# Chunk states of a scan layer from three products of rounded parts, with GpSimd's work for a chunk reordered

## The chip, the cores and the metric

The kernel runs on one core of a Trainium2 chip. The metric is device time in microseconds (us) of one execution of the whole program; lower is better. The engines of the core are called as the profile calls them: PE (TensorE, matrix products), PEld (its weight loads), DVE (VectorE), ACT (ScalarE), POOL (GpSimd) and SP (SyncE, which issues most DMAs). Each engine works through its own queue of instructions in order and waits for others by semaphores.

## The reference

A decoder trunk of two layers on 1040 tokens (16 meta tokens and 1024 inputs) of width 1024. The first layer is a Mamba-2 scan mixer and a gated FFN, the second an attention and a gated FFN. The change lies in the scan mixer. With chunks of the sequence, per group g of 8 heads (4 groups, 32 heads of 64 columns, a state of 128):

```python
xdt = x_c * dt_c[..., None]
y_diag = einsum('bgcls,bgecls,bcsgep->bclgep', cb, decay_in, xdt)
decay_to_end = exp(a_cs[..., -1:] - a_cs)
chunk_states = einsum('bclgn,bgecl,bclgep->cbgepn', b_c, decay_to_end, xdt)
def step(state, inp):
    s_new, d = inp
    return state * d[..., None, None] + s_new, state
y_off = einsum('bclgn,cbgepn,bgecl->bclgep', c_c, prev_states, exp(a_cs))
y = y_diag + y_off
```

In words: within a chunk every token takes up the earlier ones through a decay (`y_diag`); each chunk leaves a state, the product of `b_c` with its inputs times `dt` times the decay to the end of the chunk (`chunk_states`); the state that came into a chunk is read by the queries `c_c` times a decay (`y_off`).

## The kernel before

Everything is float32. Large products are made of three products of rounded parts: a value is split into a high part of type float32r and a low part (the value less its high part), and `mm3` adds high x high, high x low and low x high in one PSUM bank. In the trace these are lines 209, 210 and 211. A product of two float32 tiles that is given to PE directly shows as two records of one instruction.

The sequence is cut into 9 chunks of 116 tokens (the last of 112), and for the projections into 3 token tiles of 348, 348 and 344. The scan runs group by group (0 to 3), and in a group chunk by chunk, in `mixer`. Between the two halves of a chunk's work stand **units** of the input projections: one unit is one block of 128 output columns for one token tile, 24 products on PE. `next(work)` issues a unit. How many units go to a chunk is in `SHARES`: two in groups 0 and 3 (with exceptions at the first and last chunk), four, three and three in turn in groups 1 and 2. A block has three units; ahead of its first unit the next block's weights are split, by a copy on ACT (L196) and four subtractions on POOL (`wl`, L102). A unit of the convolved columns is evicted by ACT (L336) and then by three taps on DVE (L339), and a unit later by a Silu on ACT (L616). A unit of the gate columns is evicted by a Silu on ACT (L648), multiplied in on DVE (L655), and squared a unit later (ACT L660, DVE L664 or L666). Units write in turn to two banks `mm` and one bank `ex`.

For PE, DVE, ACT and POOL the order of all this is the order in which the Python code issues it (`manual_schedule`). Per chunk it is:

- `ssd_decays` (L735), a generator in three steps for the *next* chunk: the DMAs of its decays `D` and `E` by SP; then eight subtractions on DVE (L754) and an Exp on ACT (L755); then, but for chunk 0, `E` times the queries on POOL in four pieces (`E`, L102). Each `next(work)` but the first of a chunk takes one more step, so that with two units the DMAs and the Exp are issued among the units, and with three units the POOL step as well. What is left is taken when the next chunk begins.
- `ssd_front` (L761): on PE a transpose and a product into `cb` (L771, L772) and four transposes into `px` (L775); on ACT the copy `bk` (L780); on DVE `cbm` (L782), `xdt` (L784) and `D*cbm` (L785); on POOL the decayed inputs `xde` in two pieces (L102).
- the units.
- `ssd_back` (L791): on PE the chunk states `S` from `bk` and `xde` (L801), then for each head the products with `D` (L812) and with `E` and the incoming state (L814); on DVE the addition to the state (L807) and the skip connection (L816); on POOL the state times the next chunk's decay (`state`, L102).

The ninth chunk has no `S`, `bk` and `xde`: 32 chunks have them.

Of the kernel before, what the change touches and what calls it, by code (L numbers as in the profile page):

```python
# [8 lines left out]
F32 = mybir.dt.float32  # L9
F32R = mybir.dt.float32r  # L10
AF = mybir.ActivationFunctionType
ALU = mybir.AluOpType

P = 128
# [7 lines left out]
CH = [(c * CB, min(CB, L - c * CB)) for c in range(9)]  # L22
# [32 lines left out]
GH = 8  # L55
# [36 lines left out]
def pieces(eng, out, x, y, op):  # L92

    n = out.shape[1]
    size = 1
    for d in out.shape[2:]:
        size *= d
    step = max(1, PIECE // size)
    done = []
    for a in range(0, n, step):  # L100
        c = slice(a, min(a + step, n))
        done.append(eng.tensor_tensor(out[:, c], x[:, c], y[:, c], op=op))  # L102
    return done


class Trunk:
# [628 lines left out]
    def ssd_decays(self, g, ct, c, pool):  # L735

        nc = self.nc
        h0 = GH * g
        t0, n = CH[c]
        cc = 3 * (c % 3) + c // 3  # L740
        dk = pool.tile([P, 1024], F32, tag="D", name=self.nm("D"))
        dk = dk[:n, : GH * CB].rearrange("p (h l) -> p h l", h=GH)
        nc.sync.dma_start(dk, self.acs_d[c, h0 : h0 + GH].unsqueeze(0).to_broadcast([n, GH, CB]))
        dk = dk[:, :, :n]
        ce = None
        if c:
            ce = pool.tile([P, GH * CB], F32, tag="E", name=self.nm("E"), bufs=2)
            ce = ce.rearrange("p (h l) -> p h l", h=GH)
            nc.sync.dma_start(ce, self.ea_d[c, h0 : h0 + GH].unsqueeze(0).to_broadcast([P, GH, CB]))
            ce = ce[:, :, :n]  # L750
        yield dk, ce

        for i in range(GH):
            nc.vector.tensor_scalar(dk[:, i], dk[:, i], self.cols[:n, 1, cc, h0 + i : h0 + i + 1], 0.0, op0=ALU.subtract, op1=ALU.min)  # L754
        nc.scalar.activation(dk, dk, AF.Exp)  # L755
        yield
        if c:
            pieces(nc.gpsimd, ce, ce, ct[:, t0 : t0 + n].unsqueeze(1).to_broadcast([P, GH, n]), ALU.mult)
        yield

    def ssd_front(self, g, x, bt, ct, c, dk, pool):  # L761

        nc = self.nc
        h0 = GH * g
        tt = nc.vector.tensor_tensor
        t0, n = CH[c]
        cc = 3 * (c % 3) + c // 3
        e = t0 + n
        pcb = self.sm("cb")
        if c < 8:  # L770
            nc.tensor.transpose(pcb[:n, P : 2 * P], bt[:, t0:e], self.ident)  # L771
        nc.tensor.matmul(pcb[:n, :n], bt[:, t0:e], ct[:, t0:e], start=True, stop=True)  # L772
        px = self.lg("px")
        for q in range(4):
            nc.tensor.transpose(px[:n, q * P : q * P + P], x[q][:, t0:e], self.ident)  # L775
        px = px[:n].rearrange("p (h d) -> p h d", h=GH)
        bk = xde = None
        if c < 8:
            bk = pool.tile([P, P], F32, tag="bk", name=self.nm("bk"), bufs=2)
            nc.scalar.activation(bk[:n], pcb[:n, P : 2 * P], AF.Copy)  # L780
        cbm = pool.tile([P, CB], F32, tag="cbm", name=self.nm("cbm"), bufs=2)
        tt(cbm[:n, :n], pcb[:n, :n], self.past[:n, :n], op=ALU.mult)  # L782
        xdt = pool.tile([P, GH, 64], F32, tag="xdt", name=self.nm("xdt"), bufs=2)
        tt(xdt[:n], px, self.cols[:n, 0, cc, h0 : h0 + GH].unsqueeze(2).to_broadcast([n, GH, 64]), op=ALU.mult)  # L784
        tt(dk, dk, cbm[:n, :n].unsqueeze(1).to_broadcast([n, GH, n]), op=ALU.mult)  # L785
        if c < 8:
            xde = pool.tile([P, GH, 64], F32, tag="xde", name=self.nm("xde"), bufs=2)
            pieces(nc.gpsimd, xde[:n], xdt[:n], self.cols[:n, 2, cc, h0 : h0 + GH].unsqueeze(2).to_broadcast([n, GH, 64]), ALU.mult)
        return xdt, xde, bk

    def ssd_back(self, g, x, c, dk, ce, xdt, xde, bk, states, pool):  # L791

        nc = self.nc
        h0 = GH * g
        t0, n = CH[c]
        cc = 3 * (c % 3) + c // 3
        e = t0 + n
        state, new = states
        if c < 8:
            ps = self.lg("S")  # L800
            nc.tensor.matmul(ps, bk[:n], xde[:n].rearrange("p h d -> p (h d)"), start=True, stop=True)  # L801
            psv = ps.rearrange("p (h d) -> p h d", h=GH)
            if c == 0:
                new = pool.tile([P, GH, 64], F32, tag="state", name=self.nm("state"), bufs=2)
                nc.scalar.activation(new, psv, AF.Copy)
            else:
                nc.vector.tensor_tensor(new, new, psv, op=ALU.add)  # L807
        py = self.sm("y")
        for i in range(GH):
            q, r = i // 2, 64 * (i % 2)  # L810
            y = py[r : r + 64, q * CB : q * CB + n]
            nc.tensor.matmul(y, xdt[:n, i, :], dk[:, i, :], start=True, stop=c == 0)  # L812
            if c:
                nc.tensor.matmul(y, state[:, i, :], ce[:, i, :], start=False, stop=True)  # L814
        for q in range(4):
            nc.vector.scalar_tensor_tensor(x[q][:, t0:e], x[q][:, t0:e], self.par("d_skip", 4 * g + q),  # L816
                                           py[:, q * CB : q * CB + n], op0=ALU.mult, op1=ALU.add)
        scaled = None
        if c < 7:
            scaled = pool.tile([P, GH, 64], F32, tag="state", name=self.nm("state"), bufs=2)  # L820
            cn = 3 * ((c + 1) % 3) + (c + 1) // 3
            pieces(nc.gpsimd, scaled, new, self.cd[:, cn, h0 : h0 + GH].unsqueeze(2).to_broadcast([P, GH, 64]), ALU.mult)
        return new, scaled

    def mixer(self, mx):


        with self.tc.tile_pool(name="start", bufs=3) as pool:
            u, dt, heads, w0, front = self.load_x(pool, mx, self.a["w_in"][DI // P])
# [8 lines left out]
        with self.tc.tile_pool(name="ssd", bufs=3) as pool:  # L838
# [27 lines left out]
            with self.tc.manual_schedule(engines={E.PE, E.DVE, E.Activation, E.Pool}):  # L866
                ahead = self.ssd_decays(0, rows[0][5], 0, pool)
                dk, ce = next(ahead)
                for g in range(GROUPS):
                    *x, bt, ct = rows[g]  # L870
                    share, given = SHARES[g], 0
                    state = None, None
                    for c in range(9):
                        if g == c == 0:
                            next(work)
                            given = 1
                        for _ in ahead:
                            pass
                        begun = False
                        ops = self.ssd_front(g, x, bt, ct, c, dk, pool)  # L880
                        now = dk, ce
                        for _ in range(sum(share[: c + 1]) - given):
                            next(work)
                            if not begun:
                                begun = True
                                nxt = (g, ct, c + 1) if c < 8 else (g + 1, rows[g + 1][5], 0) if g < 3 else None
                                ahead = self.ssd_decays(*nxt, pool) if nxt else iter([(None, None)])
                                dk, ce = next(ahead)
                            else:
                                next(ahead, None)  # L890
                            given += 1
                        state = self.ssd_back(g, x, c, *now, *ops, state, pool)
                        if g == 3:
                            done.append(c)
                            todo, waiting[:] = waiting[:], []
                            for w in todo:
                                later(*w)
                            if c == 7:
                                self.gate_factors()
                                y0 = self.fetch_y(yd[0])  # L900
                next(work)
                r = [self.tmp("r0") for _ in TT]
                for t, (s0, n) in zip(r, TT):
                    self.nc.sync.dma_start(t[:, :n], self.gr_d[0:1, s0 : s0 + n].to_broadcast([P, n]))
                y0 = y0, [self.Q("yh", F32R) for _ in y0]
                for j in range(3):
                    self.split_y(0, *y0, j, r[j])
                    next(work, None)
                for _ in work:
                    pass  # L910
# [1156 lines left out]
```

## Time and profile before

| | |
|---|---|
| median of 3 runs | 2845.09 us (2844.49 to 2850.29) |
| the profiled execution's own time | 2848.77 us |
| its span, from first to last instruction | 2847.0 us |
| mean granted clock of PE | 0.997 |
| PE busy | 2806.7 us |
| DVE, ACT, POOL busy | 2071.6, 1582.8, 1572.9 us |
| `S` (L801), records and mean of one | 64, 598 ns |
| the scan's groups, from first to last `S` | 122.57 to 596.41 us |

How to read its lines. In a timeline a line has the start in us from the span's start, the time in us, the engine, the line of code and the operation, the tile that is written and those that are read (`S<-xde,bk`), the shapes, and a count when several like it are taken together; in square brackets stands how long the engine had been idle before it, and what ended that. Line 102 is the helper that cuts POOL's work into pieces, lines 209 to 211 are `mm3`: there the tile's name says which work it is. The type that is printed for products of rounded parts is f32 too. `ACT_TABLE_LOAD` loads the table of the function that the line names. In a view by stretches the columns are the stretch, its length, the busy us (and instructions) of PE, PEld, DVE, ACT and POOL, the granted clock, the share of the DMA engines and GB/s. In a view of waits a line has the engine and what it was about to do, what it waited for, the sum in us, how often, and the longest.

### The profile page before, as it was taken

The numbers are of one execution on the slowest core, as the hardware profiler recorded it, in microseconds if no ns is written. First come the engines' busy times: TensorE is split into PE (matmuls) and PEld (weight loads), VectorE is DVE, ScalarE is ACT, GpSimd is POOL, SyncE is SP. The second block draws the span as 40 slices with busy tenths as digits, with TensorE's granted clock in tenths as the row PEclk, the third lists the DMA queues.
The fourth block names the chain that finished last, engine by engine and source line by source line (L and its number), as shares of the span: only waits on it lengthen the run. The fifth ranks groups of instructions, "written<-read, shape, count | busy, mean of one in ns | idle before, by whom it ended". The sixth has DMA issues, their size and how long they took to land. (4 is left out here: it accounts for less than half of the span.)

```text
span 2847.0 us, 56457 instructions
## 1 busy us (share of the span) xinstructions
PE 2806.7 (99%) x21251; PEld 2690.8 (95%) x21251; DVE 2071.6 (73%) x3936; ACT 1582.8 (56%) x3077; POOL 1572.9 (55%) x2144
## 2 busy tenths in 40 slices
PE   8999999999999999999999999999999999999998
PEld 7989999999999999999999999999898999999888
DVE  5676666668487676767886888888759676667786
ACT  5555554543256565655335777777646555555433
POOL 2366455553519888867763111112354888886881
PEclk9999999999999999999999999999999999999999
DMA  4333333343412222235142222322532222225331
GB/s 119 88 112 97 116 84 124 117 137 101 116 68 95 78 79 79 78 129 181 44 153 75 77 67 71 85 70 55 186 132 82 83 75 82 75 83 185 111 104 67
DMA packets 141740, 281.78 MB, mean 99 GB/s; under 512 B 16307, under 2 KB 71740, under 8 KB 141468
## 3 DMA queue, kind: packets, MB, share of 16 engines
q1 hardware_dynamic: 135844, 267.01, 29.6%
q0 software_dynamic: 2048, 6.49, 0.6%
q10 hardware_dynamic: 3576, 4.67, 0.5%
q8 instruction: 168, 2.75, 0.4%
q14 instruction: 104, 0.85, 0.1%
HBM read 207.79 MB, written 55.42 MB: 92 GB/s over the span
## 5 line engine op out<-in xcount | busy, mean ns | idle before, releaser
L102 POOL TENSOR_TENSOR wl<-w,wh 128x256 fp32r<-128x256 f32 x760 | 676.3, 921 | 345.4 <-ACT wh L196 225.8
L209 PE MATMUL pj<-uh,wh 128*128 128x348 f32 (+2 forms) x1536 | 501.1, 327 | 3.4 <-DVE xbc L339 1.4
L210 PE MATMUL pj<-ul,wh 128*128 128x348 f32 (+2 forms) x1536 | 494.8, 322 | 0.8 <-DVE ul L320 0.8
L211 PE MATMUL pj<-uh,wl 128*128 128x348 f32 (+2 forms) x1536 | 491.9, 320 | 0.0
L209 PE MATMUL p<-bh,fh 128*128 128x262 f32 (+1 forms) x1408 | 401.6, 285 | 7.1 <-DVE p L1239 3.7
L211 PE MATMUL p<-bh,fl 128*128 128x262 f32 (+1 forms) x1408 | 401.4, 285 | 0.9 <-POOL fl L102 0.9
L210 PE MATMUL p<-bl,fh 128*128 128x262 f32 (+1 forms) x1408 | 399.6, 284 | 0.1
L102 POOL TENSOR_TENSOR fl<-x,fh 128x256 fp32r<-128x256 f32 x352 | 263.6, 783 | 192.9 <-ACT fh L1176 167.0
L210 PE MATMUL p<-bl,wh 128*128 128x262 f32 (+1 forms) x1040 | 295.6, 284 | 1.1 <-DVE bl L1100 1.1
L209 PEld LDWEIGHTS pj<-uh,wh 128*128 128x128 f32 x1536 | 288.7, 188 | 7.5 <-DVE qs L1607 3.1
L209 PE MATMUL p<-bh,wh 128*128 128x262 f32 (+1 forms) x1040 | 295.4, 284 | 0.4 <-ACT ft L1236 0.4
L211 PE MATMUL p<-bh,wl 128*128 128x262 f32 (+1 forms) x1040 | 294.3, 283 | 0.0
L210 PEld LDWEIGHTS pj<-ul,wh 128*128 128x128 f32 x1536 | 289.2, 188 | 2.4 <-DVE ul L320 1.4
L339 DVE SCALAR_TENSOR_TENSOR c<-p,params,c 128x260 f32<-128x260 f32 (+1 forms) x528 | 248.4, 480 | 57.4 <-ACT c L336 50.9
L211 PEld LDWEIGHTS pj<-uh,wl 128*128 128x128 f32 x1536 | 288.7, 188 | 0.1
L209 PEld LDWEIGHTS p<-bh,fh 128*128 128x128 f32 x1408 | 268.5, 191 | 8.1 <-DVE p L1239 4.1
L211 PEld LDWEIGHTS p<-bh,fl 128*128 128x128 f32 x1408 | 267.6, 190 | 1.7 <-POOL fl L102 1.3
L210 PEld LDWEIGHTS p<-bl,fh 128*128 128x128 f32 x1408 | 268.4, 191 | 0.5 <-DVE bl L1100 0.3
L1236 ACT ACTIVATE ft<-p 128x262 f32<-128x262 f32 (+1 forms) x352 | 133.6, 382 | 180.9 <-DVE p L1239 110.9
L210 PE MATMUL acc<-gl,wh 128*128 128x260 f32 (+1 forms) x672 | 214.2, 320 | 0.0
L211 PE MATMUL acc<-gh,wl 128*128 128x260 f32 (+1 forms) x672 | 213.2, 319 | 0.0
L209 PE MATMUL acc<-gh,wh 128*128 128x260 f32 (+1 forms) x672 | 210.8, 320 | 0.1
(337 smaller groups left out, 7689.2 us busy)
## 6 DMA issues: line engine op xcount, KB each, us to landing
w<-in_w_up SPq DMA_DIRECT2D x88, 512.0 KB
w<-in_w_down SPq DMA_DIRECT2D x44, 512.0 KB
w<-in_w_in SPq DMA_DIRECT2D x40, 512.0 KB
E<-ea_d SPq DMA_DIRECT2D x32, 464.0 KB
D<-acs_d SPq DMA_DIRECT2D x32, 420.5 KB
g<-c SPq DMA_DIRECT2D x88, 130.0 KB
g<-c SPq DMA_DIRECT2D x88, 128.0 KB
b<-g SPq DMA_DIRECT2D x16, 520.0 KB
```

The costliest lines, as they stand in the source:

```text
L102: done.append(eng.tensor_tensor(out[:, c], x[:, c], y[:, c], op=op))
L209: self.behind(mm(out, wh, uh, start=first, stop=False, skip_group_check=joins), tie, "behind the sums of squares")
L210: mm(out, wh, ul, start=False, stop=False, skip_group_check=joins)
L211: self.last_mm = mm(out, wl, uh, start=False, stop=last, skip_group_check=joins)
L339: ins = nc.vector.scalar_tensor_tensor(out, ps[:, o + i : o + i + n], wcol(i), out, op0=ALU.mult, op1=ALU.add)
L1236: nc.scalar.activation(s[:, :N], ps[:, :N], AF.Copy)
```

## The change

The chunk states' product of two float32 tiles becomes three products of rounded parts. `bk` becomes two tiles side by side, a high part from ACT and a low part from DVE; `xde` is split after POOL has made it, by a copy on ACT and a subtraction on DVE (`split_xde`). The buffers of `bk` and `xde` go from two to one each, with one for each part. Besides, `ssd_decays` now tells when its Exp has been issued; what is left of it when a chunk begins, POOL's `E`, is issued after `ssd_front`, so after `xde`, and not before. If the Exp is still outstanding then, that step is taken first.

```diff
@@ ssd_decays
         nc.scalar.activation(dk, dk, AF.Exp)
-        yield
+        yield "decays"
         if c:
             pieces(nc.gpsimd, ce, ce, ct[:, t0 : t0 + n].unsqueeze(1).to_broadcast([P, GH, n]), ALU.mult)
         yield
@@ ssd_front
         if c < 8:
-            bk = pool.tile([P, P], F32, tag="bk", name=self.nm("bk"), bufs=2)
-            nc.scalar.activation(bk[:n], pcb[:n, P : 2 * P], AF.Copy)
+            bk = pool.tile([P, 2, P], F32R, tag="bk", name=self.nm("bk"), bufs=1)
+            nc.scalar.activation(bk[:n, 0], pcb[:n, P : 2 * P], AF.Copy)
+            tt(bk[:n, 1], pcb[:n, P : 2 * P], bk[:n, 0].bitcast(F32), op=ALU.subtract)
...
         if c < 8:
-            xde = pool.tile([P, GH, 64], F32, tag="xde", name=self.nm("xde"), bufs=2)
-            pieces(nc.gpsimd, xde[:n], xdt[:n], self.cols[:n, 2, cc, h0 : h0 + GH].unsqueeze(2).to_broadcast([n, GH, 64]), ALU.mult)
+            xde = [pool.tile([P, GH, 64], dt, tag=t, name=self.nm(t), bufs=1) for t, dt in (("xdh", F32R), ("xdl", F32R), ("xde", F32))]
+            pieces(nc.gpsimd, xde[2][:n], xdt[:n], self.cols[:n, 2, cc, h0 : h0 + GH].unsqueeze(2).to_broadcast([n, GH, 64]), ALU.mult)
+            self.split_xde(xde, c)
         return xdt, xde, bk
+
+    def split_xde(self, xde, c):
+
+        hi, lo, t = (t[: CH[c][1]] for t in xde)
+        self.nc.scalar.activation(hi, t, AF.Copy)
+        self.nc.vector.tensor_tensor(lo, t, hi.bitcast(F32), op=ALU.subtract)
@@ ssd_back
             ps = self.lg("S")
-            nc.tensor.matmul(ps, bk[:n], xde[:n].rearrange("p h d -> p (h d)"), start=True, stop=True)
+            hi, lo = (t[:n].rearrange("p h d -> p (h d)") for t in xde[:2])
+            self.mm3(ps, bk[:n, 0], bk[:n, 1], hi, lo, True, True)
@@ mixer
                 dk, ce = next(ahead)
+                decayed = False
...
-                        for _ in ahead:
-                            pass
-                        begun = False
-                        ops = self.ssd_front(g, x, bt, ct, c, dk, pool)
+                        if not decayed:
+                            next(ahead)
+                        begun = False
+                        ops = self.ssd_front(g, x, bt, ct, c, dk, pool)
+                        for _ in ahead:
+                            pass
...
                                 dk, ce = next(ahead)
+                                decayed = nxt is None
                             else:
-                                next(ahead, None)
+                                decayed |= next(ahead, None) == "decays"
```

## Prediction

> **What bounds the kernel now.** I read the head of the page first, then the busy time by stretches, then the waits of PE, and last the timelines of single chunks.
>
> ```profile
> span 2847.0 us, 56457 instructions
> PE 2806.7 (99%) x21251; PEld 2690.8 (95%) x21251; DVE 2071.6 (73%) x3936; ACT 1582.8 (56%) x3077; POOL 1572.9 (55%) x2144
> ```
> ```profile
> 119.00:220.00 101.00, 98.50 (x775) 90.20 (x774) 77.84 (x197) 60.45 (x81) 61.85 (x85) 1.00 0.36 104
> 510.00:612.00 102.00, 101.57 (x787) 93.03 (x787) 64.33 (x158) 54.67 (x83) 71.99 (x96) 1.00 0.39 121
> ```
> ```profile
> PE y L812 <- DVE D L785: 1.5, 1, 1.5
> PE S L801 <- POOL xde L102: 1.5, 3, 0.6
> ```
>
> PE is busy for 99% of the span, at a granted clock of 1.00, so time saved on PE is time saved, and time that PE waits is time lost. The second view gives, for two stretches, length and then PE, PEld, DVE, ACT and POOL; 119 to 220 us is the scan's group 0, 510 to 612 is group 3. No other engine is near full there: DVE is at 77% and 63%, ACT at 60% and 54%. But the third view (PE alone, 115 to 612 us) says that PE does wait a little on the chain which this change lengthens: three times for the decayed inputs `xde`. So the question is not how busy ACT, DVE and POOL are, but how long the chain through them is against what PE does meanwhile.
>
> **The product itself.** One chunk in group 0, and a product of rounded parts with the same 512 columns elsewhere:
>
> ```profile
> 178.95 1.02 PE L801 MATMUL S<-xde,bk 116*128 116x512 f32 x2
> 179.90 0.43 PE L812 MATMUL y<-D,xdt 116*64 116x116 f32 x4
> ...
> 190.22 1.02 PE L801 MATMUL S<-xde,bk 116*128 116x512 f32 x2
> ```
> ```profile
> 2604.50 0.40 PE L209 MATMUL acc<-gh,wh 128*128 128x512 f32 x1
> 2604.73 0.40 PE L210 MATMUL acc<-gl,wh 128*128 128x512 f32 x1
> ```
>
> The f32 product of chunk states holds PE for 179.90 - 178.95 = 0.95 us. Products of rounded parts follow each other at 2604.73 - 2604.50 = 0.23 us, so three hold it for about 0.70. That is 0.25 us less per chunk, for 4 groups of 8 chunks 32 x 0.25 = 8.0 us: the whole possible gain. (If the change-over to the products behind costs the three the same 0.05 us as the old pair, it is 0.20 a chunk, 6.4 in all.) A chunk of group 0 now takes PE 190.22 - 178.95 = 11.27 us; after the change its own work is 11.02.
>
> **What is added, and where it stands.** Per chunk ACT gets one copy of 512 columns (the high part), queued right behind `bk`; DVE gets a subtraction from PSUM of 128 columns (the low part of `bk`), ahead of `cbm`, and one of 512 columns behind `D*cbm`. ACT's copy waits for GpSimd's `xde`, and behind it on ACT stand the next unit's evictions, Silu's table load and Silu itself: these are the ones that a late `xde` now holds up. DVE's 512 columns wait for ACT's copy, and behind them stand the next unit's taps (L339) or gate products (L655). PE's second product waits for them. (A unit is one weight block times one token tile, 24 matmuls.) The rows for the walk, group 0 first:
>
> ```profile
> 183.89 1.19 POOL L102 TENSOR_TENSOR state<-state,cd 128x256 f32<-128x256 f32 x2 [2.30 <-DVE state L807]
> 185.04 3.51 POOL L102 TENSOR_TENSOR E<-E,xbc 128x232 f32<-128x232 f32 x4
> 188.49 1.20 POOL L102 TENSOR_TENSOR xde<-xdt,cols 116x256 f32<-116x256 f32 x2
> ...
> 299.73 2.00 POOL L102 TENSOR_TENSOR xde<-xdt,cols 116x256 f32<-116x256 f32 x2 [0.52 <-DVE xdt L784]
> ```
> ```profile
> 175.31 0.64 ACT L336 ACTIVATE xbc<-pj,params 128x344 f32<-128x344 f32 x1 [2.22 <-PE pj L211]
> 175.97 1.28 ACT L616 ACT_TABLE_LOAD   x1
> ...
> 177.67 1.04 ACT L196 ACTIVATE wh<-w 128x1024 fp32r<-128x1024 f32 x1
> 179.15 0.64 ACT L336 ACTIVATE xbc<-pj,params 128x348 f32<-128x348 f32 x1 [0.44 <-PE pj L211]
> ```
> ```profile
> 179.82 1.81 DVE L339 SCALAR_TENSOR_TENSOR xbc<-pj,params,xbc 128x348 f32<-128x348 f32 x3 [2.04 <-ACT xbc L336]
> 181.55 1.60 DVE L754 TENSOR_SCALAR D<-D,cols 116x116 f32<-116x116 f32 x8
> 183.06 0.68 DVE L807 TENSOR_TENSOR state<-state,S 128x512 f32<-128x512 f32 x1
> 183.66 1.07 DVE L816 SCALAR_TENSOR_TENSOR xbc<-xbc,params,y 128x116 f32<-128x116 f32 x4
> 184.65 0.28 DVE L782 TENSOR_TENSOR cbm<-cb,past 116x116 f32<-116x116 f32 x1
> 184.83 0.69 DVE L784 TENSOR_TENSOR xdt<-px,cols 116x512 f32<-116x512 f32 x1
> ```
>
> Now `xde` runs behind the four `E` pieces and is done at 188.49 + 1.20 = 189.69, half a microsecond ahead of the product at 190.22. With the new order (it takes effect only in groups 0 and 3, two units a chunk; with three units `E` is already made before) `xde` starts when `xdt` ends, 185.5. There it runs beside DVE's `D*cbm`: the row at 299.73 is that case, 2.00 us instead of 1.20. So 187.5 instead of 189.7: 2.2 us earlier, and the two new steps come behind it. `E` follows, 3.5 us, and its last piece is wanted only by the last of the products with the queries.
>
> Unknown prices: the 512-column copy lies between this view's L648 for 348 columns, 0.46, and L196 for 1024, 1.04; by slope 0.60, and I take 0.63 with its start. The 512-column subtraction lies between L655's 0.51 and 1.00 (rows below, 348 columns, POOL idle and POOL busy) and their stretch to 512 columns, 0.75 to 1.4; since `E` runs beside it I take 0.9. The 128-column one is like `cbm`: 184.83 - 184.65 = 0.18. Below nothing none can go, each being an added instruction.
>
> On an unlagged chunk these steps fit: 187.5 + 0.6 + 0.9 = 189.0, product possible at 190.0. But ACT's queue has become part of a **ring** that leads from one `xdt` to the next, and the ring can be longer than PE's 11.02. Step by step: `xdt` 0.74 with its hand-over; `xde` 2.00; copy 0.68; ACT's L336, table load and Silu, 177.67 - 175.31 = 2.36; the second unit's L336 up to DVE's start, 179.82 - 179.15 = 0.67; three taps 181.55 - 179.82 = 1.73; L754 183.06 - 181.55 = 1.51; L807 0.60; L816 0.99; low `bk` 0.18; `cbm` 0.18. Sum 11.64. Besides, the weight split's copy L196 (1.04) stands in two chunks of three: 12.34. Today the ring is open, because ACT waits for PE (2.22 us in the row at 175.31) and its table load hides in that time; the copy waiting ahead of it takes this cover away, so that the 1.28 us come behind `xde`.
>
> Group 0 then goes at 12.34 instead of 11.27: 7 gaps between its 8 products x 1.07 = 7.5 us, less about 0.5 for idle time at the start: **+7**.
>
> Group 3, gates instead of taps:
>
> ```profile
> 522.90 1.94 POOL L102 TENSOR_TENSOR xde<-xdt,cols 116x256 f32<-116x256 f32 x2 [0.33 <-DVE xdt L784]
> 527.37 1.02 PE L801 MATMUL S<-xde,bk 116*128 116x512 f32 x2
> ...
> 561.28 1.02 PE L801 MATMUL S<-xde,bk 116*128 116x512 f32 x2
> 572.36 1.12 PE L801 MATMUL S<-xde,bk 116*128 116x512 f32 x2
> ```
> ```profile
> 561.84 0.48 ACT L660 ACTIVATE z<-xbc 128x348 f32<-128x348 f32 x1
> ...
> 566.42 1.28 ACT L648 ACT_TABLE_LOAD   x1
> 568.77 0.46 ACT L648 ACTIVATE z<-pj 128x344 f32<-128x344 f32 x1 [1.07 <-PE pj L211]
> ```
> ```profile
> 563.20 0.51 DVE L655 TENSOR_TENSOR xbc<-xbc,z 128x348 f32<-128x348 f32 x1
> 563.62 1.60 DVE L754 TENSOR_SCALAR D<-D,cols 116x116 f32<-116x116 f32 x8
> ...
> 570.27 1.00 DVE L655 TENSOR_TENSOR xbc<-xbc,z 128x344 f32<-128x344 f32 x1
> ```
>
> Ring: 0.74 + 2.00 + 0.68; table load 1.30; first unit's L648 to the end of its L655, 571.27 - 568.77 = 2.50; second unit's L660 to L754, 563.62 - 561.84 = 1.78; then 1.51 + 0.60 + 0.99 + 0.36. Sum 12.46, with a third of L196 12.8; with L655 at 0.51, 12.0 to 12.3. I take 12.4, against 572.36 - 561.28 = 11.08 today. This group starts with room: `xde` was done 527.37 - 524.84 = 2.53 ahead of its product, and ACT has a wait for PE in it. I let the first three gaps go free and four pay 1.3: **+5**.
>
> Groups 1 and 2 have three or four units a chunk:
>
> ```profile
> 249.59 0.46 ACT L648 ACTIVATE z<-pj 128x348 f32<-128x348 f32 x1 [3.48 <-PE pj L211]
> ```
> ```profile
> 251.80 1.74 POOL L102 TENSOR_TENSOR xde<-xdt,cols 116x256 f32<-116x256 f32 x2
> ```
> ```profile
> 256.88 1.02 PE L801 MATMUL S<-xde,bk 116*128 116x512 f32 x2
> ```
>
> Here the room between `xde` and product is 256.88 - 253.54 = 3.34 us, in one of the tightest chunks, and copy and subtraction take 0.6 + 0.9. The cost that is hidden here is on ACT: L648 at 249.59 would have to wait for the copy, until about 254.2, 4.6 us. PE does not feel that: a unit writes one of three banks in turn (two of `mm`, one of `ex`), so the bank is wanted again only two units (2 x 3.8 us) and a chunk's own products later. Were this cover gone, each such chunk would lose those us. So these 16 chunks gain: 16 x 0.25 = **-4**.
>
> **Sum:** +7 + 5 - 4 = +8 us. The profiled execution took 2848.77 us, 1.8 us above its span and 3.7 above the median of the runs (2845.09). From the median: 2845 + 8 = **2853 us**. Own range of this case: a copy of 0.5 to 1.0 and L655's two prices move each ring by some 0.4 us, over 11 gaps 4.4; the rings closing a chunk earlier or later is 1.3 each; the dearer subtraction (1.4) adds a little above: 2848 to 2862.
>
> [...] The table load is the largest cover that goes. In the row at 175.97 it takes 1.28 us, and L336, load and Silu together are over 2.36 us after they began, so that nothing stands behind the load. [...]
>
> **Rivals.**
> - *The ring does not close.* If `xde` beside `D*cbm` takes 1.20 instead of 2.00 (as at 188.49) and the table load still hides (Silu's load ahead of the waiting copy), the ring of group 0 is 12.34 - 0.80 - 1.28 = 10.3, under 11.02, that of group 3 likewise, and all 32 chunks gain: 2845 - 7.5 = 2837.5. For it: DVE and ACT are idle a quarter of the time or more. Against it: the rows of `xde` that begin as `xdt` ends, 2.00 at 299.73 and 1.94 at 522.90, and loads that stand directly ahead of the function that needs them.
> - *Break-even.* `xde` alone at 1.20, or L196 hidden beside DVE's work: rings of 11.5 and 11.6, +2 in each group, -4: 2845. For it: L196 in group 3 can lie beside L666 and L655.
> - *The products with the queries wait for the whole of `E`.* After the change `E` ends 3.5 us after `xde`; products with the state begin at 0.6 + 0.9 + 0.47 + 0.25 = 2.2 us after it. By pieces they never wait; if all four are waited for, 1.3 us more in each of 14 chunks: +18, about 2870. It decides as soon as one wait covers all pieces. Against: the pieces are separate instructions on separate heads.
> - *The order does not change:* `xde` stays behind `E`. The ring grows by 3.5 - 0.8 = 2.7 us in 14 chunks: +38, about 2890.
> [...]
>
> **How the numbers follow.** 0.2% (5.7 us) is about what a measurement of this kernel can tell from no change: bounds 2839.4 and 2850.8. Chances: forecast 0.50, not closed 0.22, break-even 0.18, whole `E` 0.06, order 0.02, second wait 0.02. Of the forecast's 0.50, 0.10 lies under 2850.8. So slower 0.40 + 0.10 = 0.50, same 0.18 + 0.10 = 0.28, faster 0.22. The range goes from the not-closed case's 2837 to 2864, which takes in the forecast's own range and leaves out the last three rivals and a little below.
>
> **What would show it.** Right: products S as three of L209 to L211, 0.70 us from first to next; gaps of S in group 0 of 11.7 to 12.4 us, in the later chunks of group 3 of 12 to 13; PE waiting there for ACT's high and DVE's low part, 12 to 20 us in total; `xde` at 2.00 directly behind `xdt`, `E` behind it; ACT's table load directly behind the copy; in groups 1 and 2 no wait of PE and 0.25 us less a chunk. Wrong: gaps of 11.0 in group 0, then the ring has a member that runs beside another; waits of PE in groups 1 and 2, then the banks are no cover; or waits of the state products for `E`.

## The result and the profile after

The changed kernel takes **2871.11 us** (median of 5 runs, 2869.72 to 2873.35), the kernel before beside it 2844.49 (2844.31 to 2850.29): ratio 1.0091, 95% interval 1.0080 to 1.0103. It is slower, as forecast, but by 26.6 us, where +8 was forecast, and above the range's upper end of 2864.

The head of the page after, and PE's waits in the scan (110 to 640 us):

```profile
span 2869.2 us, 56648 instructions
PE 2814.6 (98%) x21283; PEld 2703.3 (94%) x21283; DVE 2109.0 (74%) x4000; ACT 1595.9 (56%) x3109; POOL 1575.2 (55%) x2144
```
```profile
PE S L210 <- DVE xdl L797: 5.5, 11, 0.7
PE pj L209 <- DVE xbc L339: 5.1, 2, 2.5
PE S L209 <- ACT xdh L796: 4.6, 7, 1.3
PE y L821 <- DVE D L786: 3.4, 1, 3.4
PE ms L676 <- DVE z L666: 1.5, 2, 1.0
PE ms L676 <- DVE xbc L825: 0.6, 1, 0.6
```

PE now waits 20.7 us where it waited 3.0: for the two parts of `xde` (10.1), but also at three kinds of place of which the prediction had nothing: twice for DVE's taps ahead of a unit (`pj`), once for `D*cbm` (`y`), and three times, once each in groups 1 to 3, for the sums of squares `ms`.

The starts of `S` in the timelines show where. One row per stretch, us, for both kernels and for the experiments below (e7, which adds waits to the kernel before, is read by itself):

| stretch | before | after | e1 | e2 | e3 | e4 | e5 | e6 | e8 | e9 | e10 |
|---|---|---|---|---|---|---|---|---|---|---|---|
| group 0, first to last S | 78.92 | 86.07 | 76.91 | 78.62 | 85.98 | 78.07 | 99.52 | 82.12 | 78.91 | 84.17 | 89.82 |
| on to group 1's first | 26.59 | 31.41 | 27.26 | 29.11 | 31.18 | 28.65 | 29.92 | 30.03 | 26.60 | 31.72 | 27.07 |
| groups 1 and 2 | 260.02 | 268.41 | 257.53 | 257.53 | 268.59 | 260.03 | 269.44 | 267.45 | 257.55 | 267.83 | 273.49 |
| on to group 3's first | 29.00 | 28.82 | 28.83 | 28.83 | 28.99 | 29.00 | 28.83 | 28.79 | 28.85 | 28.83 | 32.67 |
| group 3, first to last S | 79.31 | 85.45 | 78.46 | 81.69 | 85.35 | 78.45 | 94.47 | 85.95 | 79.30 | 85.31 | 92.16 |

Before to after: +7.2, +4.8, +8.4, -0.2, +6.1, together +26.3. Groups 0 and 3 lose what was forecast (+7 and +5). The other 13 us stand in groups 1 and 2 and at the change from group 0 to group 1.

A chunk of group 0 after the change, by engine (POOL, ACT, DVE):

```profile
195.35 1.94 POOL L102 TENSOR_TENSOR xde<-xdt,cols 116x256 f32<-116x256 f32 x2 [0.76 <-DVE xdt L785]
197.25 3.04 POOL L102 TENSOR_TENSOR E<-E,xbc 128x232 f32<-128x232 f32 x4
```
```profile
197.32 0.63 ACT L796 ACTIVATE xdh<-xde 116x512 fp32r<-116x512 f32 x1 [3.50 <-POOL xde L102]
197.86 0.62 ACT L336 ACTIVATE xbc<-pj,params 128x348 f32<-128x348 f32 x1
198.50 1.28 ACT L616 ACT_TABLE_LOAD   x1
```
```profile
197.98 1.12 DVE L797 TENSOR_TENSOR xdl<-xde,xdh 116x512 fp32r<-116x512 f32 x1 [1.74 <-ACT xdh L796]
199.03 3.62 DVE L339 SCALAR_TENSOR_TENSOR xbc<-pj,params,xbc 128x348 f32<-128x348 f32 x6
202.56 1.60 DVE L754 TENSOR_SCALAR D<-D,cols 116x116 f32<-116x116 f32 x8
```

As forecast, `xde` starts as `xdt` ends and takes 1.94, ACT stands 3.50 us idle at the copy, and L336 and the table load come behind it. The other queue was named in the prediction, but not added up: DVE stands 1.74 us idle at its own new step, and when that is done, the taps of *two* units (`x6`) follow without a gap and lead straight to L754. Both queues are held, not ACT's alone.

PE at such a place, the high part's wait and the low part's:

```profile
198.00 0.50 PE L209 MATMUL S<-xdh,bk 116*128 116x512 f32 x1 [0.58 <-ACT xdh L796]
199.16 0.50 PE L210 MATMUL S<-xdl,bk 116*128 116x512 f32 x1 [0.66 <-DVE xdl L797]
```

And the unforeseen place in group 1, a chunk of four units of convolved columns:

```profile
336.09 0.63 ACT L796 ACTIVATE xdh<-xde 116x512 fp32r<-116x512 f32 x1 [4.54 <-POOL xde L102]
336.63 0.62 ACT L336 ACTIVATE xbc<-pj,params 128x344 f32<-128x344 f32 x1
```
```profile
336.76 0.69 DVE L797 TENSOR_TENSOR xdl<-xde,xdh 116x512 fp32r<-116x512 f32 x1 [1.74 <-ACT xdh L796]
337.37 3.59 DVE L339 SCALAR_TENSOR_TENSOR xbc<-pj,params,xbc 128x344 f32<-128x344 f32 x6
```
```profile
339.30 0.40 PE L209 MATMUL pj<-uh,wh 128*128 128x348 f32 x1 [2.54 <-DVE xbc L339]
```

The first unit's bank is read by ACT's L336 and then by three taps on DVE, and only the last of them sets it free; they end near 339.2, and the fourth unit, which takes the same bank, has been waiting for 2.54 us. Before, the first unit's taps of this chunk stood here:

```profile
315.94 1.80 DVE L339 SCALAR_TENSOR_TENSOR xbc<-pj,params,xbc 128x344 f32<-128x344 f32 x3 [0.35 <-ACT xbc L336]
```

They began 8.3 us behind the last `S` ahead of them (307.66); after the change it is 15.7 us (337.37, `S` at 321.67). Group 2 has the same place at 489.56. These two chunks take 4.1 us more each (23.07 and 23.06 between their starts of `S`, where it was 18.94), and two others 1.0 and 0.6 more, where PE waits for `ms`; the other gaps are a little shorter.

Last, the granted clock. Stretches of after, columns as before, the clock third from the end:

```profile
135.80:149.50 13.70, 13.03 (x90) 12.07 (x91) 10.94 (x26) 8.42 (x12) 10.10 (x14) 0.88 0.40 103
149.50:161.10 11.60, 11.27 (x92) 10.42 (x90) 8.78 (x23) 5.97 (x10) 7.66 (x12) 1.00 0.53 125
...
321.70:344.70 23.00, 20.46 (x139) 19.64 (x139) 19.32 (x40) 10.80 (x17) 13.83 (x20) 0.93 0.27 85
...
573.50:587.00 13.50, 12.83 (x90) 11.84 (x91) 9.29 (x23) 7.99 (x11) 8.08 (x11) 0.87 0.32 84
```
```profile
215.00:230.00 15.00, 11.56 (x81) 10.99 (x80) 11.97 (x36) 5.68 (x7) 2.36 (x5) 0.77 0.59 133
```

Before, the clock was 1.00 all through the scan. Now five stretches lie below, each behind a wait of PE, or behind two waits close together (0.70 and 0.67 us up to 136.95, 1.03 and 0.66 up to 574.67); the fifth, 471 to 495 us, has 0.93 as well. Length times missing share: 1.6 + 3.5 + 1.6 + 1.7 + 1.8 = 10 us, of which 0.6 lie inside the wait of 3.4 us itself (0.83 from 217.8 to 221.3 us). The last `S` starts 27.8 us later than before (624.23 and 596.41): the 26.3 of the table, and 1.5 ahead of the first `S`. The sum of this is: 17.7 more of waits, 9.6 of clock outside the waits, 32 x 0.16 = 5 less for the product (0.16 a chunk, from e1 below), together 22. The rest is about what the view's idle time leaves out of the delay of a start: at 199.16 the start is 1.16 us behind the one before, where 0.23 is the pace and 0.66 is listed, so 0.27 is missing; 20 more waits at that would make 5.4, an estimate from this one place.

The two profiled executions differ by 22.2 us only. Behind the scan's end, at 661 us of the kernel before, the same product of PE comes 27.7 us later after the change; at 2153 us it is 26.8 us, and 4.6 of these go up to 2212 us, where the execution of before had clock drops of its own (0.83 to 0.93 in 2160 to 2210 us, in three stretches of 10 us; after has one). The medians differ by 26.6.

### The profile page after: what moved, and what is told of

Its sections match the earlier page's. It is cut to its first block, busy times and chain, and to the rows that moved or that the text cites. A ratio compares the mean times of both kernels' runs of the same rounds, so it can differ in the third digit from the quotient of the medians.

```text
span 2869.2 us, 56648 instructions
## 1 busy us (share of the span) xinstructions
PE 2814.6 (98%) x21283; PEld 2703.3 (94%) x21283; DVE 2109.0 (74%) x4000; ACT 1595.9 (56%) x3109; POOL 1575.2 (55%) x2144
## 4 chain that ended last, share of the span: by engine, by line
PE 77%; DVE 11%; ACT 5%; POOL 3%; issue 3%; DMA 1%; DVEq 0%; ACTq 0%; POOLq 0%
PE p L211 10%; PE p L209 10%; PE p L210 10%; PE acc L209 8%; PE acc L211 8%; PE acc L210 8%; PE pj L209 4%; PE pj L210 4%; PE pj L211 4%; PE po L1725 2%; DVE D L754 2%; DVE kp L1679 2%; PE wT L1702 2%; PE lg L1668 2%; DVE xbc L339 1%
## 5 line engine op out<-in xcount | busy, mean ns | idle before, releaser
L210 PE MATMUL p<-bl,wh 128*128 128x262 f32 (+1 forms) x1040 | 295.8, 284 | 1.1 <-DVE bl L1113 1.1
L209 PE MATMUL p<-bh,wh 128*128 128x262 f32 (+1 forms) x1040 | 295.8, 284 | 0.4 <-ACT ft L1249 0.4
```

The lines of the kernel that those rows point to most:

```text
L209: self.behind(mm(out, wh, uh, start=first, stop=False, skip_group_check=joins), tie, "behind the sums of squares")
L210: mm(out, wh, ul, start=False, stop=False, skip_group_check=joins)
```

## The experiments

The theory after this reading: the loss comes from *where* copy and subtraction stand, at the head of ACT's and DVE's queues, ahead of the evictions, while `xde` isn't ready; PE's waits come from that, and the clock drops from the waits. Rivals: the product itself, the amount of added work, the new order of GpSimd, one queue alone.

### e1: three products, no split

```diff
-            xde = [pool.tile(...) for ("xdh", F32R), ("xdl", F32R), ("xde", F32)]
+            xde = [pool.tile([P, GH, 64], F32R, tag="xdh", ...)] * 3
-            self.split_xde(xde, c)
```

> Left out: the split of the decayed inputs. GpSimd writes them as a rounded tile, which takes the place of both parts, so the chunk states are not exact; PE's three products, the low part of bk and the order stay. Theory (ACT's copy waits at the head of its queue for xde, and PE's waits and the clock drops behind them come from that): no wait of PE over 0.6 us in the scan, 0.25 us less per chunk, 2844.5 - 8 = about 2837 us. Rival (three products with 116 rows and 512 columns are no cheaper than one f32 product, or their weights' loads show): 2844 or more, with 0.95 us or more from S to y.

Measured: 2842.33 us, ratio 0.9984 (0.9975 to 0.9994). Faster, so the product is not the loss; but it gains less than expected. A product of e1, where nothing waits:

```profile
242.39 0.40 PE L209 MATMUL S<-xdh,bk 116*128 116x512 f32 x1
242.63 0.39 PE L210 MATMUL S<-xdh,bk 116*128 116x512 f32 x1
242.85 0.40 PE L211 MATMUL S<-xdh,bk 116*128 116x512 f32 x1
243.18 0.33 PE L820 MATMUL y<-D,xdt 116*64 116x116 f32 x2
```

From S to y it is 243.18 - 242.39 = 0.79 us, not 0.70: three at 0.23 and 0.1 more to change over to the next product. So 0.95 - 0.79 = 0.16 us a chunk; groups 1 and 2 show (260.02 - 257.53) / 15 = 0.17. Besides, one wait for `D*cbm` stays at the end of group 0 (2.3 us).

### e2: the same work, issued behind the first unit

```diff
-            self.split_xde(xde, c)            # in ssd_front
...
                             next(work)
                             if not begun:
                                 begun = True
+                                if c < 8:
+                                    self.split_xde(ops[1], c)
```

> The whole change, but the split (ACT's copy and DVE's subtraction of 512 columns) is issued behind the first unit's evictions and not ahead of them. Same work, same number of instructions. Theory (place in the queue): xde is ready when ACT gets to the copy, so the ring opens, table load hidden again; 2835 to 2840 us. Rival (the amount of work added to ACT and DVE, 0.6 and 0.9 us a chunk): time stays within 5 us of 2871.

Measured: 2848.21 us, ratio 1.0007 (0.9997 to 1.0016). With every instruction of the change in it, 23 of the 26.6 us are gone: the place, not the amount, and not the single buffers of `bk` and the parts, which e2 has too. PE's waits:

```profile
PE y L820 <- DVE D L786: 2.4, 1, 2.4
PE S L210 <- DVE xdl L796: 2.3, 5, 0.7
PE S L209 <- ACT xdh L795: 1.9, 3, 1.3
```

Groups 1 and 2 are as in e1. The expected gain (2835 to 2840 us) is missed: in group 3 copy and subtraction still come late for the product now and then (81.69 against 78.46), and the wait for `D*cbm`, 2.42 us, costs with its clock drop 2.5 us at the change of groups. (In e1 that wait is 2.30 us with the clock at 1.00 behind it, and costs 0.7.)

### e3: the split made, but PE doesn't use it

```diff
-            self.mm3(ps, bk[:n, 0], bk[:n, 1], hi, lo, True, True)
+            nc.tensor.matmul(ps, bk[:, 0].bitcast(F32)[:n], xde[2][:n]..., start=True, stop=True)
```

> The split stays in its place, but PE takes the chunk states in one product from xde itself in f32 (from the high part of bk, so they are not exact), so PE waits for neither part. Theory (ring through ACT's queue): the ring still closes through xde, L336 and the table load, and groups 1 and 2 still wait for banks, so 2860 to 2872 us. Rival (PE waits because the parts come late for the product alone): 2845 to 2848.

Measured: 2872.96 us, a little above the expected range, ratio 1.0094 (1.0079 to 1.0109): slow as the change, stretch by stretch. PE's waits have only changed their name:

```profile
PE S L810 <- POOL xde L102: 6.1, 8, 1.5
PE pj L209 <- DVE xbc L339: 4.3, 2, 2.2
PE y L821 <- DVE D L786: 4.2, 1, 4.2
```

So it is the ring through the queues that sets the pace, whichever of its members PE waits for last. In e3 the clock is 1.00 all through groups 0 (124 to 210 us) and 3 (510 to 625 us), and they take as long as after the change, which has a stretch at half clock in each. So these two stretches, 3.4 of the 10 us, are not shown to add to the time; the likely reason is that PE would wait there without them.

### e4 and e5: the order alone, and the change without it

e4 is the kernel before with the diff of `mixer` and the `yield "decays"` alone; e5 is the change with the loop over `ahead` put back in front of `ssd_front`.

> The kernel before with the new order of GpSimd's work alone. Theory: only the waits of PE for xde (1.5 us) go, 2841 to 2845. Rival (the order itself costs, E now late for the products with the state): slower by 5 us or more, with waits of PE for E.

> The change without its new order: E before xde again, the rest as changed. Theory (ring through ACT's queue, which E lengthens by 3.5 us and shortens by xde's 0.7): gaps of S in groups 0 and 3 go from some 12.3 to 14 us or more, and the time by 25 to 45 us over the change's 2871, to 2896 to 2916. Rival (the order gains nothing, the copy's place is all): within 5 us of 2871.

Measured: e4 2845.32 us, ratio 1.0002 (0.9992 to 1.0012); e5 2893.53 us, ratio 1.0167 (1.0149 to 1.0186). The order costs nothing by itself and gains nothing measurable: it wins 0.85 us each in groups 0 and 3 and loses 2.1 at the change of groups, where `D*cbm` holds PE for 1.94 us and a stretch at half clock follows; without it the change would lose 22 us more, a little less than the 25 to 45 expected. One line of e5's waits says where:

```profile
PE S L209 <- ACT xdh L796: 23.7, 11, 3.5
```

### e6: the table load ahead of the wait

```diff
         hi, lo, t = (t[: CH[c][1]] for t in xde)
+        self.nc.scalar.activation(self.tf, self.one, AF.Silu)
         self.nc.scalar.activation(hi, t, AF.Copy)
```

> The change with a Silu of one column ahead of ACT's copy, so that the table load stands ahead of the wait for xde. One more instruction on ACT per chunk (0.2 us), the place of the copy stays. Theory (the table load is a link of the ring): about 1.05 us less per gap in groups 0 and 3, with fewer clock drops: 2855 to 2863. Rival (the load is not on the path, the copy's wait alone holds the evictions): 2869 to 2874.

Measured: 2868.28 us, ratio 1.0079 (1.0065 to 1.0092). A miss: 3 us, not 8 to 16. Group 0 gets shorter by 4, group 3 not at all. Why can be read in group 0 of e6 (ACT, then DVE; lines are one higher):

```profile
193.15 0.63 ACT L798 ACTIVATE xdh<-xde 116x512 fp32r<-116x512 f32 x1 [1.97 <-POOL xde L102]
193.69 0.62 ACT L337 ACTIVATE xbc<-pj,params 128x348 f32<-128x348 f32 x1
194.22 0.48 ACT L617 ACTIVATE xbc<-xbc 128x348 f32<-128x348 f32 x1
194.60 0.63 ACT L337 ACTIVATE xbc<-pj,params 128x344 f32<-128x344 f32 x1
```
```profile
193.82 1.15 DVE L799 TENSOR_TENSOR xdl<-xde,xdh 116x512 fp32r<-116x512 f32 x1 [1.74 <-ACT xdh L798]
194.88 3.50 DVE L340 SCALAR_TENSOR_TENSOR xbc<-pj,params,xbc 128x348 f32<-128x348 f32 x6
198.31 1.60 DVE L755 TENSOR_SCALAR D<-D,cols 116x116 f32<-116x116 f32 x8
```

ACT is done with both units' evictions by 195.2, but DVE's six taps and L755 go on as before. The table load is a link of one ring; beside it runs another through DVE alone: subtraction 1.06, six taps 3.43 (194.88 to 198.31), then the same steps to `xdt`.

### e9 and e10: one queue at a time

In e9 GpSimd makes the high part (two casts right behind `xde`), so that ACT is out of it; in e10 ACT's copy stays in its place and only DVE's subtraction is issued behind the first unit.

> The change with the high part made by GpSimd, right behind xde, and not by ACT: ACT waits for nothing of GpSimd any more, DVE's subtraction stays in its place behind D*cbm, some 0.6 us later. Theory (both queues are held, ACT's by the copy and DVE's by the subtraction with six taps behind it): DVE's queue alone keeps the ring of group 0 at 11.5 to 12.1 us a chunk, 2858 to 2875. Rival (ACT's queue alone makes the loss): 2840 to 2850.

> The change with ACT's copy in its place and DVE's subtraction behind the first unit's taps or gate products: DVE waits for nothing of ACT's copy any more but through the evictions that follow it. Theory (both queues are held): ACT's queue alone, with L196, the table load and the eviction behind the copy, keeps most of the loss, 2855 to 2870. Rival (DVE's queue alone makes the loss): 2840 to 2850.

Measured: e9 2869.44 us, ratio 1.0088 (1.0071 to 1.0104); e10 2886.35 us, ratio 1.0148 (1.0133 to 1.0163). Each queue alone is enough for the loss: e9 has DVE's alone, and e10 differs from e2 only in the place of ACT's copy (2886.35 against 2848.21 us). A chunk of e9 (ACT, DVE):

```profile
179.80 0.64 ACT L336 ACTIVATE xbc<-pj,params 128x344 f32<-128x344 f32 x1 [0.38 <-PE pj L211]
```
```profile
183.61 1.16 DVE L798 TENSOR_TENSOR xdl<-xde,xdh 116x512 fp32r<-116x512 f32 x1 [1.77 <-POOL xdh L797]
184.69 3.50 DVE L339 SCALAR_TENSOR_TENSOR xbc<-pj,params,xbc 128x344 f32<-128x344 f32 x6
```

ACT evicts at 179.80, as soon as PE is done, yet the taps of that unit start 4.9 us later, behind the subtraction. e10 was outside its range upwards: there the subtraction stands behind the eviction and taps of a unit that ACT itself has made late, so the two delays come one behind the other, and PE waits 27 us for the low part alone. So e10 shows what the place of ACT's copy does, but not by the path of the change itself. And in groups 1 and 2 the loss of e9 is as large as that of the change, but made up otherwise: PE waits 4.1 us there for the low part and 1.9 for taps, where the change has 5.1 for taps.

### e7: waits made on purpose

```diff
+            for i in range(DELAY.get((g, c), 0)):      # 12 to 21, in six chunks of groups 1 and 2
+                nc.gpsimd.tensor_tensor(idle, idle, idle, op=ALU.add)
             pieces(nc.gpsimd, xde[:n], xdt[:n], ...)
```

> The kernel before, with idle additions on GpSimd (0.6 us each, 12 to 21 of them) ahead of xde in six chunks of groups 1 and 2, so that PE waits once there for a time of its own, by estimate some 1 to 4 us. Theory (a wait of PE of over some 2 us is followed by a stretch at half clock, of a few us, whatever caused it): the longer waits are each followed by a stretch of 3 us or so with products at twice their spacing, and cost 1.5 us more than the wait; the short ones are not. Rival (the half clock belongs to the new product or to DMA traffic): spacing unchanged after every wait.

Measured: 2881.36 us in its one run, and six waits of PE, from 1.8 to 6.0 us. Each window starts with the product that had waited, for 3.3, 3.8, 4.6, 6.0, 1.8 and 3.1 us in this order:

```profile
246.90:264.70 17.80, 17.77 (x113) 15.98 (x114) 8.97 (x22) 5.80 (x11) 8.99 (x12) 0.82 0.32 81
288.00:307.00 19.00, 18.95 (x116) 16.75 (x117) 8.51 (x19) 5.33 (x9) 14.22 (x22) 0.84 0.60 212
346.00:364.00 18.00, 17.92 (x113) 16.13 (x114) 8.20 (x21) 4.55 (x7) 13.83 (x21) 0.83 0.36 109
416.90:433.50 16.60, 16.55 (x113) 14.91 (x114) 8.72 (x22) 3.40 (x7) 8.99 (x12) 0.89 0.27 87
454.80:471.20 16.40, 16.35 (x117) 15.04 (x118) 10.78 (x24) 6.20 (x11) 15.15 (x24) 1.00 0.67 237
508.50:525.00 16.50, 16.50 (x112) 15.27 (x113) 8.35 (x20) 4.56 (x7) 13.68 (x20) 0.90 0.40 120
```

Behind the wait of 1.8 us the clock stays at 1.00; behind the five of 3.1 us and more it is lower, and 1.7 to 3.2 us are lost on top (0.10 x 16.5, 0.18 x 17.8). Waits (22.5 us) and lost clock (12.8) together are about what groups 1 and 2 take longer than before (295.8 and 260.0 us between the same starts of `S`). No new product and no split are in this kernel, so the drops follow from the waits. The wait of 6.0 us costs no more than 1.8 on top because the clock falls while PE still waits:

```profile
413.60:416.90 3.30, 0.00 (x0) 0.00 (x0) 0.24 (x1) 3.00 (x4) 3.06 (x7) 0.50 0.00 0
```

The waits of all these kernels in the scan do not give one length from which the clock falls. Every wait of 2.8 us and more is followed by half clock (15 of them); of those between 1.7 and 2.6 us 18 are and 7 are not. One of each, behind a wait of 2.55 us in e6 (up to 334.47) and behind one of 1.72 us in e10 (up to 177.39):

```profile
334.50:337.90 3.40, 3.40 (x21) 3.40 (x22) 3.33 (x6) 1.63 (x2) 3.40 (x7) 1.00 0.07 23
...
177.40:182.00 4.60, 4.60 (x39) 3.94 (x40) 4.47 (x16) 1.87 (x2) 1.19 (x3) 0.63 0.34 116
```

Two shorter waits a microsecond apart can do it as well: the two pairs named above did, and a third, 0.58 and 0.66 us up to 199.16, did not. What is alike is the length: in the scan a stretch at 0.50 is 3.4 us long (339.6 to 343.0 after the change, 4.6 x 0.37 = 1.7 us lost in e10), or twice that (220.1 to 226.9). In slices of 10 us the drops of all these kernels lose 1.7 to 1.8 us each or 3.4 to 3.5 (clock 0.83 from 190 to 200 us in e5, 0.66 from 220 to 230 us after the change).

### e8: three products only where they fit

Groups 1 and 2 as in e2, groups 0 and 3 and the order as in the kernel before.

> Three products in groups 1 and 2 alone, with the split behind the first unit's evictions; groups 0 and 3 and the order as in the kernel before. Theory (0.16 us a chunk where no ring closes): 16 chunks x 0.16 = 2.6 us less, about 2842. Rival (ACT and DVE still delay evictions there): 2845 or more, with waits of PE for banks.

Measured: 2841.81 us, ratio 0.9989 (0.9980 to 0.9998), groups 1 and 2 at 257.55. This is the part of the change that is left when its place is put right: 2.5 us of the scan, and a little faster than both kernels.

## Why the prediction was right and wrong

- **The ring closes: right.** Direction and mechanism held: gaps of `S` in group 0 average 86.07 / 7 = 12.3 us, as worked out, and e2 and e3 show that place and ring, not work or the product's own wait, make it. PE waits 10.1 us for the two parts, where 12 to 20 were named.
- **Its members: in part.** The sum went through ACT and the table load. e6 and e9 show a second ring of nearly the same length through DVE's subtraction and six taps, which alone keeps the loss (e9). That the sum through one ring gave the length to a tenth is in part luck. The prediction named the taps as standing behind the subtraction, and then did not add up that way round. The subtraction was also dearer: 1.12 us beside `E` (0.69 alone at 336.76), where 0.9 was taken. And the table load was not hidden in the wait of 2.22 us before: in the rows at 175.31 and 175.97 it stands behind that wait; e6 took it off the path for 3 us in all.
- **Groups 1 and 2, -4: wrong, the step that failed.** "PE does not feel that: a unit writes one of three banks in turn ... so the bank is wanted again only two units ... and a chunk's own products later." This was read from a unit of gate columns, which ACT alone evicts. A unit of convolved columns holds its bank until DVE's last tap, and in a chunk of four units no chunk's products lie before the bank's next use: 2.54 us of wait at 339.30 and again in group 2. With clock and the smaller waits, those for `ms` among them, +8.4 us came instead of -4, 12 of the missing 19 us.
- **The change of groups: left out.** Chunk 8 of group 0 has one unit. Its `D*cbm` (220.22 after) came 3.4 us late for PE, where it was 1.5 late before, and 6.8 us at half clock go with it: +4.8 us. The new order alone (e4) has 2.1 of this; how much is the lag of the chunks before was not separated.
- **A wait costs more than itself: left out.** 10 us of clock lie in the stretches above, of which 6 to 7 lie where no ring sets the pace; the prediction counted waits only.
- **The product: mis-sized.** 0.16 us a chunk, not 0.25. The prediction had the change-over (0.20) as the lower value and left part of it out.
- **A second wait behind the table load (chance 0.02).** No run shows it: after the change L616's load at 198.50 ends at 199.78, and the Silu behind it starts at 199.79; in e6 the load at 189.68 ends at 190.96, and its Silu starts at 190.97.

What stays open: what decides whether a wait between 1.7 and 2.6 us is followed by half clock, and what in group 3 of e2 makes the parts late now and then.

## What to carry to other kernels

When a step is added to an engine that has time to spare, ask what it waits for and what is queued behind it: here ACT stood idle for 3.50 us ahead of its copy, with the evictions queued behind it, and issuing the same instructions one unit later gave back 23 of 26.6 us. Follow the delay on every engine that gets a new wait, and for each kind of work that holds a buffer ask which instruction sets it free. And where the matrix engine is full, price a wait above itself: here one of 2.8 us or more always brought half clock, and one of 1.7 to 2.6 us mostly, for 1.7 us or twice that.

## What the runs showed of the hardware that was not expected

- Every wait of PE of 2.8 us or more was followed by half clock (in e7 1.7 to 3.2 us lost on top of waits of 3.1 to 6.0 us), 18 of 25 between 1.7 and 2.6 us too (1.72 in e10 was, 2.55 in e6 was not), and always for 3.4 us or twice that (in slices of 10 us, 1.7 to 1.8 or 3.4 to 3.5 us lost).
- DVE's subtraction of 116 x 512 took 0.69 us alone (after the change, at 336.76) and 1.12 to 1.16 beside GpSimd's products into `E` (at 197.98 and 585.02).
- GpSimd's cast of 116 x 512 to float32r took 0.74 us in all (e9), less than its product of the same size (1.18 alone).
